# A one-core hybrid decoder layer: front order, scan pace and planner distances set anew

## The chip, the core and the metric

One core of a Trainium2 chip runs one layer. The time is that of the device in microseconds, from one launch; lower is better. PE is the matrix engine (TensorE), PEld its weight loads, DVE, ACT and POOL are the vector, scalar and general engines, and SP issues nearly all DMAs.

## The reference

The input is x with 1024 positions of 1024 values, float32. One projection by w_in feeds two mixers that run side by side; their outputs are gated, added and projected.

```python
h = rms_norm(x, norm_w)
q, k, v, z_a, xbc, z_s, dt_raw, gate_logits = split(h @ w_in)
y_a = diff_attention(q, k, v) * silu(z_a)      # 8 heads, two softmax maps of 64 dims each, causal
xs, B, C = split(silu(causal_conv4(xbc)))      # 2048 + 512 + 512 channels
y_s = ssd_chunked(xs, softplus(dt_raw), A, B, C, D)   # 32 heads, 4 groups, 8 chunks of 128
y_s = gated_group_rms_norm(y_s, z_s)
merged = sigmoid(g_a) * (y_a @ w_proj_attn) + sigmoid(g_s) * (y_s @ w_proj_ssd)
out = x + merged @ w_out
```

In the attention each map takes the row softmax of its scores, and the second, times a learned lambda, is taken from the first before the product with v. The scan carries a state of 128 x 512 per group from chunk to chunk.

## The kernel before

**Arithmetic.** Float32 accuracy comes from pairs: every operand is held as a rounded high part and a remainder, and a product is three matmuls (high x high, high x low, low x high; `steps3`, `mm3`). A weight therefore costs a load, a copy on ACT (high part) and a subtraction on DVE or POOL (low part). Large products are done by a scheme with seven block products instead of eight; it needs sums and differences of blocks of both operands.

**Stages.** The front makes what the scan needs: `FRONT_ORDER` is a string of blocks that PE works through. y is the first half of a z projection (`z_first`, tiles pmz), and "z16" one block product of the second kind of z projection (`z_part`: pair 1, product 6; tiles pz). c is a pair of 128-column blocks of the conv channels and g one of the gates (`front_pair`: PSUM banks fX, fY, fZ); e is the first part of a gate pair (`gate_first`), which makes the later g pair of the same number short (order `REST`, five products of 12 matmuls instead of seven). d is the dt projection. Then come eight heads (`att_proj`, tiles pma) with the attention blocks, then the remaining gates (pg), the output projections of both mixers (`products`: px, py, pz) and the last projection (`final`: poa to pod).

**The scan and the attention run between.** A group of the scan starts when its conv blocks (four of x, one of B, one of C) and its z rows lie in DRAM. Each chunk (`ssd_chunk`) is a chain through all engines; its PE work (px, pc, pb, pO, pS, pD, py) falls between the projection's matmuls. `qk_stack` transposes a half of a head's q and k, and `att_core` starts the blocks of 128 query rows one after another (`att_block`: scores sc, transposes pa, product av, transpose pya). The scores use 64 of the 128 rows of PE.

**What sets the order.** The program is written by a planner. `Plan` keeps a clock `pl.t` and a busy time for each engine; each piece of work is a generator that yields the time at which it wants to go on, and the projections (`bulk`) fill the rest. Every instruction is emitted when the planner's clock reaches it, so the planner's costs and distances set the order in which instructions stand on each engine, and buffers are handed out by its estimate of when they come free. On the chip each engine works through its own list in order and waits on semaphores.

**Names that the change touches.** `PACE` (line 35) is the distance between the starts of two chunks of the scan (line 1496); `ZSUMS` (line 40) gives the times at which the sums of weight blocks start (`weight_sums` on POOL: the first two for the z weights, absolute; the third for w_out, counted from the end of the heads' projections, line 2151). Line 831 starts `qk_stack` after a head's half is projected, line 900 parts two attention blocks, lines 205 and 221 to 226 hold costs of matmuls, line 235 the time until a result is out of PE, line 105 how far an engine's queue may run ahead.

**Weights of a front pair.** Four raw tiles (`rawf`, four buffers of the pool `raw`) are loaded by SP. POOL makes differences and sums of them (`s3`, `rawf`), and each of seven (five) pieces is split by ACT and DVE or POOL into a weight tile `wp`; there are nine of these. The next pair's loads can start only when the four raw buffers come free.

**Partial sums of z.** `z_part` gets `keep`: where the next block of the order is a product of the same pair, its partial sums (`zu`, `zv`, `zc`) stay in SBUF; otherwise they are stored to `zc_d` and loaded again.

Of the kernel before, what the change touches and what calls it, by code (L numbers as in the profile page):

```python
# [31 lines left out]
C_DT = 9216  # L32
C_GATE = 9248
NBIG, NW, NRAW, NMID, NSM = 17, 9, 4, 16, 8
PACE = 19.5
FRONT = 12
SLOW = 32.0
FRONT_ORDER = "y0 e6 y1 e0 e4 c6 e2 d0 c20 z06 c16 z07 z05 g0 c2 z04 c0 z16 z03 g2 z17 z15 z14 c4 z13 c8 g8 c14 g6 c22 g10 c12 g4 c10 c18"
REST = (("t2", 6), ("b22", 3), ("t3", 7), ("t1", 5), ("t4", 4))
ZSUMS = (75.0, 182.0, 11.0)  # L40
WPOOL = 3
NEARLY = 48
FINAL = (("b11", 1), ("t1", 5), ("t2", 6), ("t3", 7), ("b21", 2), ("b22", 3), ("t4", 4))
NFIN = 4 * len(FINAL)
HOP = 0.12
DBG = 0
INF = float("inf")

# [36 lines left out]
class Plan:  # L85
# [8 lines left out]
    def op(self, eng, cost, after, shared=False):  # L94
# [3 lines left out]
        if shared:  # L98
            self.e["L"] = s + cost
        return s + cost + HOP  # L100

    def spawn(self, gen, at=None):
        self.tasks.append([self.t if at is None else at, gen])

    def room(self, eng, ahead=0.2):
        while self.e[eng] > self.t + ahead:
            yield self.e[eng] - ahead

# [37 lines left out]
def tile_hybrid_layer(ctx: ExitStack, tc: tile.TileContext, x, norm_w, w_in, q_norm_w, k_norm_w,  # L146
# [29 lines left out]
    pl = Plan()  # L176
# [7 lines left out]
    def bigt(shape, dt=F32, name="b"):  # L184
        return big.tile(shape, dt, tag="b4", name=name)
# [16 lines left out]
        return hpool.tile([P, KB, S], F32R, tag="h", name=name)  # L202


    lag = [0.0135, 1.5]

    shape = [""]

    def mm(o, lhsT, rhs, start, stop, after=0.0, **kw):
        nc.tensor.matmul(o, lhsT=lhsT, rhs=rhs, start=start, stop=stop, **kw)  # L210
        n, m = rhs.free_size(), lhsT.free_size()
        now = "c" if rhs.dtype == F32 and m <= 64 else "r" if rhs.dtype != F32 and lhsT.shape[0] <= 64 else ""
        if rhs.dtype == F32:
            c = 0.058 if now else max(4 * n / 2400, 0.215)
        elif now:
            c = max(n / 4800 + lag[0] / 2, 0.0545)
        else:
            c = max(n / 2400 + lag[0], 0.057 if m <= 64 else 0.107)
        c += 0.089 * (now != shape[0])
        shape[0] = now  # L220
        pl.t = max(pl.t, after) + c

# [2 lines left out]
        pl.t = max(pl.t, after) + 0.108  # L225

    def pe_done():
        return pl.t + 0.2

    def mm3(o, ah, al, bh, bl, first, last):  # L230
        mm(o, ah, bh, first, False)
# [8 lines left out]
    def act(o, i, f, after, **kw):  # L240
        nc.scalar.activation(o, i, f, **kw)  # L241
        if f in (AF.Silu, AF.Exp) and f != table[0]:
            table[0] = f
            pl.op("A", 1.3, after)
        c = 0.83e-3 * i.free_size() + (0.052 if in_ps(i) else 0.093) + 0.093 * (("accum_out" in kw) + any(not isinstance(kw.get(i, 0.0), float) for i in ("scale", "bias")))
        return pl.op("A", c, after)

    def tt(o, a, b, op, after, eng="V"):
        (nc.vector if eng == "V" else nc.gpsimd).tensor_tensor(out=o, in0=a, in1=b, op=op)  # L249
        n = o.free_size()  # L250
        if eng == "G":
            return pl.op("G", 0.095 + (1.85e-3 if op == ALU.mult else 2.3e-3) * n, after, True)
        sb = not in_ps(a, b)
        return pl.op("V", 0.07 + 0.07 * sb + 1.042e-3 * n, after, sb)

    def stt(o, a, s, b, op0, op1, after):
        nc.vector.scalar_tensor_tensor(out=o, in0=a, scalar=s, in1=b, op0=op0, op1=op1)  # L257
        sb = not in_ps(a, b)
        return pl.op("V", 0.07 + 0.07 * sb + 1.042e-3 * o.free_size() + (0.0 if isinstance(s, float) else 0.06), after, sb)
# [105 lines left out]
    ORDER1 = []  # L365
    for e in FRONT_ORDER.split():
        ORDER1.append((e[0], int(e[1:])))
# [220 lines left out]
    def w_next(n):  # L588
        i = used[0]
        used[0] += n  # L590
        return list(range(i, i + n))
# [47 lines left out]
    def form_evac(t):  # L639
# [10 lines left out]
        def split(f, src, at):  # L650
# [6 lines left out]
            for kp in range(2):  # L657
                yield from pl.room("V")
                at = tt(forms_t[f, 1, kp][0][:, :, cs], src[:, 2 * kp:2 * kp + 2], forms_t[f, 0, kp][0][:, :, cs],
                        ALU.subtract, at - HOP if kp else at)  # L660
            ready["formed", f, t] = at
# [35 lines left out]
    def prep_h(t):  # L697
# [28 lines left out]
        for i in range(2):  # L726
            hs = slice(i * 512, i * 512 + 512)
            at = stt(xt[:, hs], xt[:, hs], rs, nwb[i], ALU.mult, ALU.mult, at - HOP if i else at)
            nt.append(at)
# [10 lines left out]
    def h_evac(t, half, pt, kt, at):  # L740
# [5 lines left out]
        if t >= 4:  # L746
# [5 lines left out]
            b = b2[t][0][:, half * 4:half * 4 + 4]  # L752
            t1 = act(b, src, AF.Copy, max(at - HOP, pl.t))
            sums12[t, half] = (b, t1)
# [39 lines left out]
    def att_proj(h):  # L794
        ids = w_next(KB)
        ks = []
        for _ in range(4):
            ks.append((yield from pl.get(heads)))
        v = bigt([P, NT, P], name=f"v{h}")
        zg = bigt([P, NT, P], name=f"zg{h}")  # L800
        kk = [bigt([P, S], F32R, name=f"kk{h}{i}") for i in range(2)]
        hd[h] = (v, zg, kk, ks)
        lefts[h] = [NT, {}]
        qk = []
        for ts in ((0, 1), (2,), (3,), (4,), (5,), (6,), (7,)):
            pms = []
            for t in ts:
                k = yield from pl.get(trs, first=True)
                pms.append((mmt(f"pma{h}{t}"), k))
                if t % 2 == 0:  # L810
                    km = yield from pl.get(qkm)
                    qk.append([midt([P, 2, 256], name=f"qk{h}{t}"), km, 0])
            if FRONT == 16 and h == HEADS - 1 and ts[0] == NT - 1:
                pl.spawn(h_done())
            for kb in range(KB):
                yield from w_need(ids[kb])
                for t, (pm, k) in zip(ts, pms):
                    yield from steps3(pm, hblk(kb, t), wide(ids[kb]), kb == 0, kb == KB - 1)
                    if kb == KB - 1:
                        pl.spawn(att_evac(h, t, pm, k, qk[-1][0][:, t % 2, :], qk[-1]), pe_done())  # L820
                if ts[0] == NT - 1:
                    w_done(ids[kb])
            if ts[-1] % 4 == 3:
                pl.spawn(qk_stack(h, ts[0] // 4, qk), pl.t + 3.0)
                qk = []

    def h_done():
# [27 lines left out]
    def qk_stack(h, half, qk):  # L855
        v, zg, kk, _ = hd[h]
        cs = slice(half * 512, half * 512 + 512)
        while len(qk[0]) < 5 or len(qk[1]) < 5 or "consts" not in ready:
            yield pl.t + 0.2
        yield max(qk[0][3:] + qk[1][3:] + [ready["consts"]])  # L860
        kq = yield from pl.get(bigs)
        q = bigt([P, 2, 512], F32R, name=f"q{h}{half}")
        done = []
        for isk in range(2):
            k = yield from pl.get(trs)
            pt = trt(f"pq{h}{half}{isk}")
            for i in range(4):
                tp(pt[:, i * P:(i + 1) * P], qk[i // 2][0][:, i % 2, isk * P:(isk + 1) * P])
            if isk:
                for c in qk:  # L870
                    qkm.give(c[1], pl.t + 0.1)
            at = pe_done()
            yield at
            if isk:
                t1 = act(kk[0][:, cs], pt, AF.Copy, at)
                yield t1
                t1 = tt(kk[1][:, cs], pt, kk[0][:, cs], ALU.subtract, t1)
            else:
                t1 = act(q[:, 0], pt, AF.Copy, at, scale=wqk_c)
                yield t1  # L880
                t1 = stt(q[:, 1], pt, wqk_c, q[:, 0], ALU.mult, ALU.subtract, t1)
            done.append(t1)
            trs.give(k, t1)
        pl.spawn(att_core(h, half, (q, kq)), max(done))

    def att_core(h, half, q):
        for qb in range(half * 4, half * 4 + 4):
            while bigs.avail(1 + half) > pl.t:
                a = bigs.avail(1 + half)
                yield a if a < INF else pl.t + 0.2  # L890
            pk = [bigs.take() for _ in range(1 + half)]
            pl.spawn(att_block(h, qb, pk, q))
            yield pl.t + 0.6

    def att_block(h, qb, pk, q):
        v, zg, kk, ks = hd[h]
# [7 lines left out]
        def soft(m):  # L904
            p = bigt([P, S], name=f"p{h}{qb}{m}") if qb >= 4 else pboth[:, m]
            nms, t1 = [], 0.0
            for i, (j, e) in enumerate(cols):
                while len(scs) <= i:
                    yield pl.t + 0.1
                sc, k, at = scs[i]  # L910
                at = max(at, t1 - HOP)
                yield at
# [40 lines left out]
        yield at  # L953
        at = stt(pr[0][:, 0:n], pr[1][:, 0:n], cc, pr[0][:, 0:n], ALU.mult, ALU.add, at - HOP)
        if qb >= 4:
# [513 lines left out]
    def ssd_core(g):  # L1469
# [20 lines left out]
        for c in range(NT):  # L1490
# [4 lines left out]
            pl.spawn(ssd_chunk(g, c, state, abs_))  # L1495
            yield pl.t + (PACE if bigs.avail(3) <= pl.t or 'setup' in ready else SLOW)

# [429 lines left out]
    def out_block(c, ob, r, h, ps, cell, at, free=None):  # L1927
# [15 lines left out]
        if c == 2 and ob >= 4:  # L1943
            mids.give(km[1], at)
            rows[ob + r - 4, h] = (gt, km[0], at)
            if DBG: print("  rows",ob+r,h,round(at,1),round(pl.t,1),"V",round(pl.e["V"],1),"G",round(pl.e["G"],1),"A",round(pl.e["A"],1))
            return
# [186 lines left out]
    def bulk():  # L2134
# [3 lines left out]
        for i in range(2):  # L2138
            pl.spawn(weight_sums(i, w_in, C_ZS + i * 1024, ZSUMS[i]))
        for n, (kind, i) in enumerate(ORDER1):  # L2140
# [9 lines left out]
        pl.spawn(fill())  # L2150
        pl.spawn(weight_sums(2, w_o, 0, pl.t + ZSUMS[2]))
        yield from gates()
# [74 lines left out]
```

## Time and profile before

| | |
|---|---|
| median of 3 runs | 1575.51 us (1575.27 to 1576.5) |
| the profiled execution | 1579.94 us |
| its span, first to last instruction | 1578.2 us |
| granted clock of PE, mean of the span | 0.995 |
| DMA | 287.46 MB, mean 182 GB/s |

The profile is one execution. Its page gives each engine's busy time, the span in 40 slices and the chain that ended last; further views group instructions, list who waited for whom, show a stretch in order of time, or sum busy times in chosen stretches. "[0.88 <-ACT wp L241]" behind an instruction says that its engine stood idle for 0.88 us before it and that ACT's write of wp ended the wait. PE's instructions overlap, so a block of equal matmuls is timed from the start of the first to the start of the next block. Nearly all matmuls are recorded under line 210, the helper `mm`.

### The profile page before, as it was taken

The numbers are of one execution on the slowest core, as the hardware profiler recorded it, in microseconds if no ns is written. First come the engines' busy times: TensorE is split into PE (matmuls) and PEld (weight loads), VectorE is DVE, ScalarE is ACT, GpSimd is POOL, SyncE is SP. The second block draws the span as 40 slices with busy tenths as digits, with TensorE's granted clock in tenths as the row PEclk, the third lists the DMA queues.
The fourth block names the chain that finished last, engine by engine and source line by source line (L and its number), as shares of the span: only waits on it lengthen the run. The fifth ranks groups of instructions, "written<-read, shape, count | busy, mean of one in ns | idle before, by whom it ended". The sixth has DMA issues, their size and how long they took to land.

```text
span 1578.2 us, 26112 instructions
## 1 busy us (share of the span) xinstructions
PE 1551.3 (98%) x8562; PEld 1256.0 (80%) x8562; DVE 1152.4 (73%) x2111; ACT 897.0 (57%) x2209; POOL 775.7 (49%) x902
## 2 busy tenths in 40 slices
PE   7989999999999999999999999999999999999999
PEld 5866888888888788778887877787878788888887
DVE  5767868577688778766778677876456687888985
ACT  7653434567555575676667666666546464443350
POOL 3264366344556553546684645464765744222005
PEclk9999999999999999999999999999999999999999
DMA  6475698753544453425473323343445797798846
GB/s 226 149 248 178 225 303 286 249 184 121 157 143 145 153 150 115 134 64 155 140 225 98 106 89 106 92 148 94 160 147 179 234 306 265 256 320 270 307 136 220
DMA packets 254825, 287.46 MB, mean 182 GB/s; under 512 B 18391, under 2 KB 162528, under 8 KB 254690
## 3 DMA queue, kind: packets, MB, share of 16 engines
q1 hardware_dynamic: 254686, 285.79, 56.3%
q8 instruction: 68, 1.11, 0.3%
q14 instruction: 67, 0.55, 0.1%
q10 hardware_dynamic: 4, 0.00, 0.0%
HBM read 196.47 MB, written 89.26 MB: 181 GB/s over the span
## 4 chain that ended last, share of the span: by engine, by line
PE 90%; ACT 3%; DMA 2%; DVE 2%; issue 1%; POOL 1%; SPq 0%; POOLq 0%; DVEq 0%; ACTq 0%
PE pma L210 22%; PE pz L210 10%; PE py L210 6%; PE fYc L210 6%; PE fXc L210 4%; PE sc L210 4%; PE av L210 4%; PE fZc L210 4%; PE px L210 4%; PE pO L210 3%; PE pg L210 3%; PE fYg L210 2%; PE pmz L210 2%; PE pa L224 2%; PE poz L210 1%; PE poy L210 1%
## 5 line engine op out<-in xcount | busy, mean ns | idle before, releaser
L210 PE MATMUL pma<-w,hH 128*128 128x512 f32 x1024 | 346.3, 407 | 0.3 <-DVE y L257 0.3
L210 PEld LDWEIGHTS pma<-w,hH 128*128 128x128 f32 x1024 | 187.0, 189 | 39.2 <-issue 4.5
L210 PE MATMUL pma<-w,hL 128*128 128x512 f32 x512 | 209.4, 409 | 0.0
L241 ACT ACTIVATE w<-raw 128x512 fp32r<-128x512 f32 (+1 forms) x166 | 101.1, 627 | 53.6 <-DMA raw<-wf_d 23.1
L249 DVE TENSOR_TENSOR w<-raw,w 128x512 fp32r<-128x512 f32 (+1 forms) x134 | 106.0, 808 | 27.6 <-ACT w L241 25.4
L210 PEld LDWEIGHTS pma<-w,hL 128*128 128x128 f32 x512 | 96.6, 189 | 21.7 <-issue 5.3
L241 ACT ACTIVATE p<-p,nm 128x256 f32<-128x256 f32 (+7 forms) x128 | 98.3, 773 | 25.8 <-DVE nm L914 24.9
L210 PE MATMUL fYc<-ft,wp 128*128 128x512 f32 x432 | 107.0, 395 | 3.5 <-DVE fu L249 1.8
L249 POOL TENSOR_TENSOR rawf<-rawf,rawf 128x512 f32<-128x512 f32 x54 | 70.7, 1310 | 79.4 <-DVE wp L249 36.2
L210 PEld LDWEIGHTS fYc<-ft,wp 128*128 128x128 f32 x432 | 81.8, 190 | 22.1 <-DVE fu L249 2.4
L210 PE MATMUL pz<-w,ft 128*128 128x512 f32 x384 | 90.3, 392 | 0.0
L241 ACT ACTIVATE wp<-rawp 128x512 fp32r<-128x512 f32 x72 | 44.3, 626 | 76.4 <-POOL rawp L249 18.8
L914 DVE CUSTOM_DVE_ANT_0 p<-sc,maskb 128x512 f32<-128x512 f32 (+3 forms) x128 | 69.8, 586 | 24.1 <-PE sc L210 24.0
L210 PEld LDWEIGHTS pz<-w,ft 128*128 128x128 f32 x384 | 71.6, 188 | 15.1 <-DVE w L249 0.4
L241 ACT ACTIVATE ab<-ab,nac 128x128 f32<-128x128 f32 x256 | 78.4, 391 | 5.0 <-POOL ab L1479 4.7
L249 POOL TENSOR_TENSOR rawp<-rawp,rawp 128x512 f32<-128x512 f32 x36 | 52.0, 1454 | 57.1 <-DVE wp L249 50.0
L249 POOL TENSOR_TENSOR os<-os,os 128x512 f32<-128x512 f32 x48 | 67.2, 1400 | 23.8 <-DMA os<-in_w_in_dram 19.6
L210 PEld LDWEIGHTS av<-v,at 128*128 128x128 f32 x576 | 72.1, 191 | 6.4 <-issue 1.5
L210 PE MATMUL av<-v,at 128*128 128x128 f32 x576 | 75.5, 276 | 0.3 <-ACT at L241 0.3
L281 POOL TENSOR_TENSOR rs<-rs,mhalf 128x4 f32<-128x4 f32 (+1 forms) x71 | 72.5, 1021 | 5.9
L945 POOL TENSOR_TENSOR rec<-s,mone 128x1 f32<-128x1 f32 x64 | 35.6, 557 | 76.9 <-ACT p L241 76.4
L210 PE MATMUL sc<-kk,q 64*128 64x512 f32 (+3 forms) x576 | 72.0, 367 | 0.0
(378 smaller groups left out, 4194.1 us busy)
## 6 DMA issues: line engine op xcount, KB each, us to landing
raw<-in_w_in_dram SPq DMA_DIRECT2D x104, 256.0 KB, 2.9
rawf<-in_w_in_dram SPq DMA_DIRECT2D x72, 256.0 KB, 3.9
ab<-act_d SPq DMA_DIRECT2D x32, 512.0 KB, 4.7
wf_d<-os SPq DMA_DIRECT2D x48, 256.0 KB, 5.1
cv_d<-cv SPq DMA_DIRECT2D x48, 256.0 KB, 3.5
raw<-wf_d SPq DMA_DIRECT2D x48, 256.0 KB, 3.6
t_d<-ts SPq DMA_DIRECT2D x24, 512.0 KB, 3.2
os<-in_w_in_dram SPq DMA_DIRECT2D x32, 256.0 KB, 4.5
```

Of the source, the lines that this page charges most:

```text
L210: nc.tensor.matmul(o, lhsT=lhsT, rhs=rhs, start=start, stop=stop, **kw)
L224: nc.tensor.transpose(out=o, in_=i, identity=ident if idn is None else idn)
L241: nc.scalar.activation(o, i, f, **kw)
L249: (nc.vector if eng == "V" else nc.gpsimd).tensor_tensor(out=o, in0=a, in1=b, op=op)
L281: nc.gpsimd.tensor_tensor(out=dst, in0=dst, in1=mhalf[:, 0:cols], op=ALU.pow)
L914: nc.vector.tensor_tensor_reduce(out=p[:, j:e], in0=sc[m][:, 0:e - j], in1=maskb[:, S - n + j:S - n + e], scale=-1.0, scalar=nms[i - 1] if ...
L945: nc.gpsimd.tensor_tensor(out=rec, in0=sums[1], in1=mone, op=ALU.pow)
```

## The change

Three tables of numbers and the front order change, and eight numbers that stood in the code get names. No matmul is added or removed.

```diff
-PACE = 19.5
+PACE = 18.0
-FRONT_ORDER = "y0 e6 y1 e0 e4 c6 e2 d0 c20 z06 c16 z07 z05 g0 c2 z04 c0 z16 z03 g2 z17 z15 z14 c4 z13 c8 g8 c14 g6 c22 g10 c12 g4 c10 c18"
+FRONT_ORDER = "y0 e6 y1 e0 e4 c6 e2 d0 c20 z06 c16 z07 z05 g0 c2 z04 c0 c10 z16 z03 g2 z17 z15 c4 z14 z13 c8 c14 g6 g8 c12 g4 g10 c22 c18"
-ZSUMS = (75.0, 182.0, 11.0)
+ZSUMS = (75.0, 182.0, 3.0)
+DONE = 0.2
+STACK = 2.0
+SPACE = 0.4
+AHEAD = 0.2
+DLAG = 1.5
+TURN = 0.089
+HALF = 0.05
-            c = 0.058 if now else max(4 * n / 2400, 0.215)
+            c = HALF if now else max(4 * n / 2400, 0.215)
-                pl.spawn(qk_stack(h, ts[0] // 4, qk), pl.t + 3.0)
+                pl.spawn(qk_stack(h, ts[0] // 4, qk), pl.t + STACK)
-            yield pl.t + 0.6
+            yield pl.t + SPACE
```

`DONE`, `AHEAD`, `DLAG` and `TURN` have the values of the numbers that they replace. `STACK` (3.0 before), `SPACE` (0.6) and `HALF` (0.058) have new ones. In the front, c10 moves from the last place but one to the place behind c0, c4 comes between z15 and z14, g8 goes behind g6, g10 behind g4, and c22 stands just ahead of c18. Each engine's list changes in order; SP's has 16 DMAs more, the partial sums of z15 that are stored and loaded again, and ACT's has two table loads less.

More of the change, by code (lines that the diff above doesn't have):

```diff
@@ L103, in spawn, with room @@
         self.tasks.append([self.t if at is None else at, gen])
-    def room(self, eng, ahead=0.2):
+    def room(self, eng, ahead=AHEAD):
         while self.e[eng] > self.t + ahead:
@@ L202, in hpt @@
         return hpool.tile([P, KB, S], F32R, tag="h", name=name)
-    lag = [0.0135, 1.5]
+    lag = [0.0135, DLAG]
     shape = [""]
@@ L218, in mm @@
             c = max(n / 2400 + lag[0], 0.057 if m <= 64 else 0.107)
-        c += 0.089 * (now != shape[0])
+        c += TURN * (now != shape[0])
         shape[0] = now
@@ L227, in pe_done @@
     def pe_done():
-        return pl.t + 0.2
+        return pl.t + DONE
     def mm3(o, ah, al, bh, bl, first, last):
```

## The prediction

> **What bounds the kernel now.** I read the page first: the busy shares, then the chain that ended last.
>
> ```profile
> span 1578.2 us, 26112 instructions
> PE 1551.3 (98%) x8562; PEld 1256.0 (80%) x8562; DVE 1152.4 (73%) x2111; ACT 897.0 (57%) x2209; POOL 775.7 (49%) x902
> PE 90%; ACT 3%; DMA 2%; DVE 2%; issue 1%; POOL 1%; SPq 0%; POOLq 0%; DVEq 0%; ACTq 0%
> ```
>
> TensorE is busy 98% of the span and nine tenths of the chain are its own instructions. The change adds and removes no matmul, so it can act in only two ways: through the time in which PE stands still, and through what a matmul loses because of the one ahead of it. The idle time is 1578.2 - 1551.3 = 26.9 us. Next I cut the span into stretches of 50 us, and then one longer stretch of the attention part.
>
> ```profile
> 0.00:50.00 50.00, 40.71 (x172) 30.64 (x173) 31.39 (x56) 38.62 (x71) 14.86 (x31) 0.93 0.62 205
> 50.00:100.00 50.00, 47.84 (x208) 38.37 (x207) 36.25 (x53) 28.73 (x66) 22.68 (x17) 1.00 0.55 181
> 100.00:150.00 50.00, 45.71 (x196) 34.20 (x195) 37.01 (x59) 16.96 (x31) 29.55 (x24) 0.97 0.72 227
> ...
> 200.00:250.00 50.00, 50.00 (x222) 41.30 (x221) 34.21 (x48) 20.35 (x37) 35.78 (x27) 1.00 0.95 313
> ...
> 500.00:550.00 50.00, 47.35 (x262) 38.40 (x261) 36.88 (x51) 26.74 (x53) 29.11 (x25) 0.97 0.47 144
> ```
> ```profile
> sum 500.00, PE 497.72 PEld 398.05 DVE 364.10 ACT 339.77 POOL 275.95; mean PE 99.54 PEld 79.61 DVE 72.82 ACT 67.95 POOL 55.19
> ```
>
> The columns are PE, PEld, DVE, ACT and POOL busy time, granted clock, DMA share and GB/s. At 200 to 250 us PE is full, 222 matmuls in 50 us. At 500 to 550 us, where the front ends, 2.65 us are missing and the clock is 0.97. The last row sums 600 to 1100 us, where attention and the scan run: 2.3 us idle in 500 us. Of the 26.9 us, 9.29 + 2.16 + 4.29 = 15.7 lie in the first 150 us, and there the PE order is unchanged: its first difference stands at the end of the block fZc0, where z16 (pz) starts at 265.78 us.
>
> ```profile
> 265.78 1.52 PE L210 MATMUL pz<-w,ft 128*128 128x512 f32 x6
> ```
>
> So what the change can win back sits around 540 us.
>
> **The stall near 540 us, the first term.** The waits of PE in 500 to 600 us, PE's timeline, and the engines that feed it:
>
> ```profile
> PE fXc L210 <- DVE wp L249: 1.8, 1, 1.8
> PE fXc L210 <- ACT wp L241: 0.9, 1, 0.9
> PE fXc L210 <- ACT fc L241: 0.5, 1, 0.5
> ```
> ```profile
> 535.16 1.15 PE L210 MATMUL pO<-xdt,ab 128*64 128x64 f32 x32
> 537.19 0.50 PE L210 MATMUL fXc<-hH,wp 128*128 128x512 f32 x1 [0.88 <-ACT wp L241]
> 537.53 0.40 PE L210 MATMUL fXc<-hL,wp 128*128 128x512 f32 x1
> 539.70 1.22 PE L210 MATMUL fXc<-hH,wp 128*128 128x512 f32 x2 [1.77 <-DVE wp L249]
> 540.72 0.63 PE L210 MATMUL fXc<-hL,wp 128*128 128x512 f32 x1
> ...
> 542.42 0.81 PE L210 MATMUL fXc<-hH,wp 128*128 128x512 f32 x2
> ...
> 549.46 2.88 PE L210 MATMUL fYc<-ft,wp 128*128 128x512 f32 x12
> 552.18 2.88 PE L210 MATMUL fZc<-ft,wp 128*128 128x512 f32 x12
> ```
> ```profile
> 530.83 2.10 SPq L270 DMA_DIRECT2D rawf<-in_w_in_dram  x4
> ```
> ```profile
> 529.75 1.29 POOL L249 TENSOR_TENSOR wp<-rawf,wp 128x512 fp32r<-128x512 f32 x1
> 535.31 1.28 POOL L249 TENSOR_TENSOR s<-rawf,rawf 128x512 f32<-128x512 f32 x1 [4.27 <-DMA rawf<-in_w_in_dram]
> ```
> ```profile
> 531.11 0.67 DVE L249 TENSOR_TENSOR fu<-fc,fYg 128x512 f32<-128x512 f32 x1
> 535.27 0.69 DVE L249 TENSOR_TENSOR fc<-fc,fYg 128x512 f32<-128x512 f32 x1 [0.41 <-PE fYg L210]
> 538.97 0.67 DVE L249 TENSOR_TENSOR wp<-rawf,wp 128x512 fp32r<-128x512 f32 x1
> ```
> ```profile
> 540.00:545.00 5.00, 5.00 (x19) 3.99 (x19) 1.43 (x3) 3.54 (x7) 3.69 (x5) 0.72 0.14 52
> ```
>
> This is the pair c10, behind the short gate pair g4. A short pair has five products of 12 matmuls instead of seven. The four raw buffers come free only when POOL has split g4's last piece (529.75); then the loads of c10 are issued (530.83 to 532.93) and land from 535.3. The lower half of c10's first weight is written at 538.97, behind four other DVE rows that follow g4's last sum (535.27), and PE starts in earnest at 539.70. A steady matmul takes (552.18 - 549.46)/12 = 0.227 us. The two gaps are 0.88 + 1.77 = 2.65 us. Behind them six matmuls take 542.42 - 539.70 = 2.72 us instead of 6 x 0.227 = 1.36: the clock row (0.72) shows why. The stall costs 2.65 + 1.36 = **4.0 us**.
>
> The Trainium skill, "TensorE: Matmul & The Clock Gate", section "What's actually happening", says the clock halves after about one idle window of 3.4 us, windows running freely. This trace shows the halving after two gaps of 0.88 and 1.77 us with two matmuls between. By the rule's letter the stall would cost 2.65 us alone.
>
> The new front order takes c10 out of this place and runs it right behind c0. PE, before and then now, at c0's end (fXc10 is c10's first bank, pz61 the products z16):
>
> ```order
> L210 MATMUL fZc0_2358<-hL_115,wp81_2367 128x512
> L210 MATMUL fZc0_2358<-hH_114,wp81_2367 128x512
> L210 MATMUL pz610_2532<-w48_2421,ft20_204 128x512 x2
> L210 MATMUL pz610_2532<-w48_2421,ft22_206 128x512
> L210 MATMUL pz610_2532<-w49_2430,ft20_204 128x512 x2
> L210 MATMUL pz610_2532<-w49_2430,ft22_206 128x512
> ```
> ```order
> L217 MATMUL fZc0_2358<-hL_115,wp81_2367 128x512
> L217 MATMUL fZc0_2358<-hH_114,wp81_2367 128x512
> L217 MATMUL fXc10_2519<-hH_114,wp82_2465 128x512
> L217 MATMUL fXc10_2519<-hL_115,wp82_2465 128x512
> L217 MATMUL fXc10_2519<-hH_114,wp82_2465 128x512 x2
> L217 MATMUL fXc10_2519<-hL_115,wp82_2465 128x512
> ```
>
> 84 matmuls of c10 move ahead of z16, about 19 us, so z16's summed weights have that much more time. What stands behind g4 now is g10. The question is whether g10 starves as c10 did. DVE shows it, before and then now: wp170 and wp163 are the first weights of the pair behind g4, and fc<-fc,fYg4 is g4's last sum.
>
> ```order
> L249 TENSOR_TENSOR fc_5031<-fc_5031,fYg4_5029 128x512
> L257 SCALAR_TENSOR_TENSOR cv1_5035<-tail_4915,cols1_109,cv1_5035 128x2
> L249 TENSOR_TENSOR pO07_5158<-pO07_5158,xn07_5042 128x512
> L257 SCALAR_TENSOR_TENSOR cv1_5035<-tail_4915,cols1_109,cv1_5035 128x3
> L249 TENSOR_TENSOR xn07_5042<-pO07_5158,zc07_5170 128x512
> L249 TENSOR_TENSOR wp170_5210<-rawf820_5147,wp170_5210 128x512
> ```
> ```order
> L256 TENSOR_TENSOR fu7_4914<-fc_4819,fYg4_4817 128x512
> L256 TENSOR_TENSOR wp163_4905<-rawf810_4832,wp163_4905 128x512
> L256 TENSOR_TENSOR fu7_4914<-fu7_4914,fZg4_4818 128x512
> L256 TENSOR_TENSOR fu6_4855<-fu6_4855,fZg4_4818 128x512
> L264 SCALAR_TENSOR_TENSOR cv1_4733<-tail_4809,cols1_109,cv1_4733 128x3
> L264 SCALAR_TENSOR_TENSOR cv1_4823<-fZc12_4610,cols1_109,cv1_4823 128x511
> L256 TENSOR_TENSOR fc_4819<-fc_4819,fYg4_4817 128x512
> ```
>
> The first weight moves from five rows behind g4's last sum to five rows ahead of it, right behind fu7<-fc. In the trace those two sums lie 535.27 - 531.11 = 4.2 us apart, so the weight should be there before g4's last product ends. c22 behind g10, the next close place, has its first weight two rows ahead of g10's last sum. I take the whole stall as gone: **-4.0 us**. The 0.5 us wait of fXc on fc I leave as it is:
>
> ```profile
> 563.11 2.45 ACT L241 ACTIVATE ab<-ab,nac 128x128 f32<-128x128 f32 x8
> ...
> 566.65 0.58 ACT L241 ACTIVATE fc<-fXc 128x512 f32<-128x512 f32 x1
> ```
>
> it comes when eight exponentials of the scan (2.45 us) stand ahead of the copy on ACT, which the new order does not exclude; bounds 0.5 either way.
>
> **Turns of the array, the second term.** The scores (sc) use 64 of the 128 rows; around each run of them PE loses time.
>
> ```profile
> 1012.27 0.39 PE L210 MATMUL pma<-w,hH 128*128 128x512 f32 x1
> 1012.59 0.97 PE L210 MATMUL sc<-kk,q 64*128 64x512 f32 x6
> 1013.48 0.50 PE L210 MATMUL pma<-w,hH 128*128 128x512 f32 x1
> ```
> ```profile
> 840.04 0.62 PE L210 MATMUL pma<-w,hH 128*128 128x512 f32 x2
> 840.59 1.67 PE L210 MATMUL sc<-kk,q 64*128 64x512 f32 x12
> 842.18 0.50 PE L210 MATMUL pma<-w,hL 128*128 128x512 f32 x1
> ```
>
> From start to start a run of 6 costs 1.21 - 0.227 = 0.98 us, a run of 12 costs 2.14 - 2 x 0.227 = 1.69. Joining two saves 2 x 0.98 - 1.69 = 0.28 us. The smaller distances of the attention blocks (0.6 to 0.4) join some runs and part others; PE's rows have 74 runs before and 69 now. One of them, head 0, before and now (sc0000 and sc0010 are the two maps of block 0, sc0100 and sc0110 those of block 1):
>
> ```order
> L210 MATMUL sc0000_6091<-kk00_5642,q00_5995 128x128
> L210 MATMUL sc0010_6092<-kk00_5642,q00_5995 128x128
> L210 MATMUL pma05_6018<-w91_5699,hH_114 128x512
> L210 MATMUL sc0100_6108<-kk00_5642,q00_5995 128x256
> L210 MATMUL sc0110_6109<-kk00_5642,q00_5995 128x256
> ```
> ```order
> L217 MATMUL sc0000_6018<-kk00_5588,q00_5922 128x128
> L217 MATMUL sc0010_6019<-kk00_5588,q00_5922 128x128
> L217 MATMUL sc0100_6027<-kk00_5588,q00_5922 128x256
> L217 MATMUL sc0110_6028<-kk00_5588,q00_5922 128x256
> L217 MATMUL sc0100_6027<-kk01_5589,q00_5922 128x256
> ```
>
> The pma row no longer parts the blocks 0 and 1. Five runs fewer at 0.28 are **-1.4 us**.
>
> **What is added, the third term.** "No instruction added" holds for PE, not for SP: c4 now stands between z15 and z14, so z15's partial sums go to DRAM and come back, 8 stores and 8 loads of 256 KB, 4.2 MB. At 313 GB/s (the row at 200 us) that is 13 us of the DMA engines, hidden beside PE's work on c4; if that cover failed, a PSUM bank would wait for its load, 3.9 us as for the weights:
>
> ```profile
> rawf<-in_w_in_dram SPq DMA_DIRECT2D x72, 256.0 KB, 3.9
> ```
>
> Partial sums already go out and come back around other z steps before, and no wait of PE names them, so I take nothing. HALF (0.058 to 0.05) is only the planner's own cost of a small matmul. The scan's pace (19.5 to 18.0), the earlier stacks (3.0 to 2.0) and the closer blocks put PE's rows nearer behind the DVE and ACT rows that they need. The trace cannot show that wait; the 2.3 us idle of 600 to 1100 us bound it: all of it may go, or it may double. I take **+1.0 us**, under half of it more, since two of the distances shrink by a third and DVE is 73% busy there. The earlier w_o sums (11.0 to 3.0 behind the last head) are read by the last stage alone: nothing.
>
> Sum: -4.0 - 1.4 + 1.0 = -4.4 us. The profiled execution took 1579.94 us (span 1578.2 and what lies around it), so 1575.5 of its kind; the median of the runs is 1575.51, 4.4 lower than the profiled one, and with the same difference it becomes **1571.1 us**. A measurement here tells about 0.2%, 3.2 us, from no change.
>
> **Rivals.** (a) The starvation moves instead of going: g8 behind g6 or g10 behind g4 waits. For it: both are still pairs behind a short pair, and a load that misses its time there stops PE at once. Against it: the DVE rows above. It gives back 2.65 to 4.0 us: 1573.8 to 1575.1. (b) The half clock is not paid in ordinary runs, or not in all: the slow stretch followed gaps of under 2 us in one execution, and the profiled one is 4.4 us above the median. Then only 2.65 is won there and the time is 1575.51 - 2.65 - 1.4 + 1.0 = 1572.5; this is also what the page's rule gives. (c) Slower: crowding of DVE in 600 to 1100 us. With the scan at 18.0 and blocks at 0.4, DVE's queue runs late by more than PE has other work for. Three gaps as long as the 1.77 us one, each with a slow stretch of 1.36, are 9.4 us and give 1575.51 - 5.4 + 9.4 = 1579.5. It decides from about 8.6 us of new loss on; DVE at 73% and 2.3 us idle now speak against it. (d) More is won: the 0.5 us of fc and the 2.3 us go too, and no wait comes: 1575.51 - 5.4 - 2.8 = 1567.3.
>
> **How the numbers follow.** Forecast 0.50, (a) 0.20, (b) 0.12, (c) 0.08, (d) 0.10. Faster by over 0.2% (below 1572.4) are the forecast and (d), 0.60; within it (a) and (b), 0.32; slower (c), 0.08. The range runs from 1566.8, just under (d), to 1576.0, above (a); (c) and the far ends are left out.
>
> **What would show it.** Right: no wait of fXc or fXg on wp of over 0.3 us between 500 and 580 us, and a granted clock of 1.00 there; PE idle in 600 to 1100 us of 2 to 5 us; shorter sums of PE idle by about 2.6 us in the front. Wrong: a new gap of over 1 us with a clock row below 0.9 anywhere behind 266 us, or a wait of PE on a bank that z14 or z13 holds while its partial sum is loaded.

## The result and the profile after

The changed kernel takes **1562.65 us** (median of 6 runs, 1562.19 to 1563.96), the kernel before 1575.24 us beside it (6 runs, 1572.81 to 1576.5). The ratio is 0.9924 (0.9912 to 0.9937): 12.6 us faster, 4.2 us beyond the fast end of the range. The profiled execution took 1562.57 us.

A word on line numbers: the changed kernel stands seven lines lower. Where the text ahead names lines 831, 900, 221 to 226 and 235, these are its lines; in the kernel before they are 824, 893, 214 to 219 and 228. In the rows below `mm` is L217, the transposes L231, ACT's copies L248, DVE's and POOL's sums L256.

The page of the changed kernel: its span, its busy times, and its chain by engine.

```profile
span 1560.8 us, 26193 instructions
PE 1540.5 (99%) x8562; PEld 1252.8 (80%) x8562; DVE 1146.5 (73%) x2113; ACT 894.3 (57%) x2207; POOL 774.9 (50%) x900
PE 95%; DMA 1%; ACT 1%; DVE 1%; issue 0%; POOL 0%; SPq 0%; DVEq 0%; ACTq 0%; POOLq 0%
```

PE's share of the chain rises from 90% to 95%; its idle time falls from 26.9 us to 1560.8 - 1540.5 = 20.3 us, and the same 8562 matmuls keep it busy for 10.8 us less. Both of these mix two things, since the first profile of the kernel before had a slow start: its clock was 0.93 in the first 50 us. A second profile of the same program (the first experiment below) starts like this, by the stretches of 50 us:

```profile
0.00:50.00 50.00, 40.06 (x181) 30.03 (x182) 34.50 (x60) 40.35 (x73) 14.92 (x31) 1.00 0.67 222
```

It did 181 matmuls there instead of 172, and its span is 1571.6 us: **6.6 us between two executions of one program**. I compare the changed kernel with this second one from here on. The busy times from 151 us to the end, of the kernel before in its second profile and then of the changed kernel:

```profile
151.00:1571.60 1420.60, 1410.67 (x7963) 1148.55 (x7961) 1043.08 (x1931) 808.81 (x2038) 709.21 (x831) 1.00 0.56 180
```
```profile
151.00:1560.80 1409.80, 1404.05 (x7961) 1147.94 (x7959) 1032.95 (x1932) 806.29 (x2035) 706.32 (x828) 1.00 0.57 185
```

The second number less the third is PE's idle time behind the start: 9.9 us before, 5.75 after. Some 3.3 us of either lie behind the last matmul, so of 6.6 us that can be won 4.2 are gone. The views of PE's waits in the same stretches say which, of the kernel before (second profile) and of the changed kernel; the columns are us in total, times, longest:

```profile
PE fXc L217 <- DVE wp L256: 1.4, 1, 1.4
PE fXc L217 <- ACT wp L248: 0.9, 1, 0.9
PE pya L231 <- DVE y L264: 0.8, 2, 0.5
PE pa L231 <- DVE p L264: 0.6, 1, 0.6
PE pod L217 <- DVE xr L264: 0.6, 1, 0.6
PE pb L231 <- ACT at L248: 0.5, 1, 0.5
PE fXc L217 <- ACT fc L248: 0.5, 1, 0.5
PE py L217 <- DVE u L256: 0.5, 1, 0.5
PE pq L231 <- DVE qk L256: 0.4, 1, 0.4
PE av L217 <- ACT at L248: 0.3, 1, 0.3
PE pma L217 <- DVE y L264: 0.3, 1, 0.3
```
```profile
PE py L231 <- ACT xn L248: 0.9, 1, 0.9
PE pod L217 <- DVE xr L264: 0.6, 1, 0.6
PE fYg L217 <- DVE fu L256: 0.5, 1, 0.5
PE pO L217 <- DVE ab L256: 0.5, 1, 0.5
```

The list shrinks from eleven rows to four. The stall of c10 (the two rows of fXc on wp) is gone and so are all waits of the attention part. The sums over 600 to 1300 us, before (second profile) and after, show the latter best:

```profile
sum 700.00, PE 697.17 PEld 561.27 DVE 488.05 ACT 451.57 POOL 406.93; mean PE 99.60 PEld 80.18 DVE 69.72 ACT 64.51 POOL 58.13
```
```profile
sum 700.00, PE 699.98 PEld 567.12 DVE 492.11 ACT 454.99 POOL 408.62; mean PE 100.00 PEld 81.02 DVE 70.30 ACT 65.00 POOL 58.37
```

Idle there: 2.83 us before, **0.02 us after**, although DVE, ACT and POOL are each a little busier. In the front, the row of the changed kernel for the place where the stall stood, and its three small new waits in PE's timeline:

```profile
500.00:550.00 50.00, 50.00 (x256) 41.26 (x256) 31.27 (x48) 28.89 (x56) 27.65 (x23) 1.00 0.47 144
```
```profile
429.06 1.15 PE L217 MATMUL pO<-xdt,ab 128*64 128x64 f32 x32 [0.48 <-DVE ab L256]
434.27 0.66 PE L231 MATMUL py<-ident,xn 128*128 128x128 f32 x4 [0.89 <-ACT xn L248]
497.65 2.56 PE L217 MATMUL fYg<-ft,wp 128*128 128x512 f32 x10 [0.49 <-DVE fu L256]
```

### The profile page after: what moved, and what is told of

Read it like the earlier page. It is cut to its first block, busy times and chain, and to the rows that moved or that the text cites. A ratio compares the mean times of both kernels' runs of the same rounds, so it can differ in the third digit from the quotient of the medians.

```text
span 1560.8 us, 26193 instructions
## 1 busy us (share of the span) xinstructions
PE 1540.5 (99%) x8562; PEld 1252.8 (80%) x8562; DVE 1146.5 (73%) x2113; ACT 894.3 (57%) x2207; POOL 774.9 (50%) x900
## 4 chain that ended last, share of the span: by engine, by line
PE 95%; DMA 1%; ACT 1%; DVE 1%; issue 0%; POOL 0%; SPq 0%; DVEq 0%; ACTq 0%; POOLq 0%
PE pma L217 23%; PE pz L217 11%; PE py L217 6%; PE fYc L217 6%; PE sc L217 4%; PE av L217 4%; PE fXc L217 4%; PE px L217 4%; PE fZc L217 4%; PE pO L217 3%; PE pg L217 3%; PE fYg L217 3%; PE pmz L217 2%; PE pa L231 2%; PE poz L217 1%; PE fZg L217 1%
## 5 line engine op out<-in xcount | busy, mean ns | idle before, releaser
L217 PE MATMUL pma<-w,hH 128*128 128x512 f32 x1024 | 344.9, 407 | 0.0
L217 PEld LDWEIGHTS pma<-w,hH 128*128 128x128 f32 x1024 | 186.2, 189 | 40.8 <-issue 6.6
L217 PE MATMUL pma<-w,hL 128*128 128x512 f32 x512 | 207.9, 406 | 0.0
L248 ACT ACTIVATE w<-raw 128x512 fp32r<-128x512 f32 (+1 forms) x166 | 100.9, 631 | 57.2 <-DMA raw<-wf_d 21.1
L256 DVE TENSOR_TENSOR w<-raw,w 128x512 fp32r<-128x512 f32 (+1 forms) x136 | 107.3, 808 | 29.0 <-ACT w L248 28.2
L217 PEld LDWEIGHTS pma<-w,hL 128*128 128x128 f32 x512 | 96.7, 189 | 20.3 <-issue 2.9
L217 PE MATMUL fYc<-ft,wp 128*128 128x512 f32 x432 | 106.1, 392 | 2.4 <-DVE ft L256 1.8
L248 ACT ACTIVATE p<-p,nm 128x256 f32<-128x256 f32 (+7 forms) x128 | 98.1, 770 | 17.8 <-DVE nm L921 15.9
L256 POOL TENSOR_TENSOR rawf<-rawf,rawf 128x512 f32<-128x512 f32 x54 | 71.8, 1329 | 64.2 <-issue 20.6
L217 PEld LDWEIGHTS fYc<-ft,wp 128*128 128x128 f32 x432 | 80.4, 188 | 20.4 <-DVE ft L256 2.2
L248 ACT ACTIVATE wp<-rawp 128x512 fp32r<-128x512 f32 x72 | 44.2, 627 | 81.7 <-PE py L217 23.5
L217 PE MATMUL pz<-w,ft 128*128 128x512 f32 x384 | 90.5, 392 | 0.3 <-DVE w L256 0.3
L256 POOL TENSOR_TENSOR os<-os,os 128x512 f32<-128x512 f32 x48 | 65.1, 1357 | 43.0 <-DMA os<-in_w_out_dram 19.5
L217 PEld LDWEIGHTS pz<-w,ft 128*128 128x128 f32 x384 | 71.6, 188 | 15.4 <-DVE w L256 0.7
L256 POOL TENSOR_TENSOR rawp<-rawp,rawp 128x512 f32<-128x512 f32 x36 | 53.2, 1491 | 53.8 <-DVE wp L256 40.1
L248 ACT ACTIVATE ab<-ab,nac 128x128 f32<-128x128 f32 x256 | 78.4, 397 | 2.2 <-POOL ab L1486 2.1
L217 PEld LDWEIGHTS av<-v,at 128*128 128x128 f32 x576 | 72.5, 191 | 5.1 <-issue 1.1
L248 ACT ACTIVATE wp<-rawf 128x512 fp32r<-128x512 f32 x100 | 60.3, 623 | 27.6 <-POOL rawf L256 24.1
L217 PE MATMUL av<-v,at 128*128 128x128 f32 x576 | 75.4, 276 | 0.0
L217 PE MATMUL sc<-kk,q 64*128 64x512 f32 (+3 forms) x576 | 70.8, 366 | 0.0
```

## The experiments

The question was where 12.6 us come from when the prediction found 4.4. The theories: the gain is the sum of its parts (front, pace, distances, sums), each worth something alone; or one part brings it; or it belongs to the order that all the numbers make together, and to no number. Each kernel computes everything. All are in the table; the idle time is PE's behind 151 us, from the same row as above (the expectations count it without the 3.3 us behind the last matmul).

| kernel | median, us | ratio to before | idle, us |
|---|---|---|---|
| before, profiled again | 1573.35, one run | | 9.9 |
| changed | 1562.65 | 0.9924 (0.9912 to 0.9937) | 5.75 |
| before + front order | 1573.89 | 1.0001 (0.999 to 1.0012) | 12.8 |
| before + pace | 1588.11 | 1.0089 (1.0073 to 1.0105) | 18.7 |
| before + distances | 1589.74 | 1.0101 (1.0085 to 1.0118) | 23.7 |
| changed, old front order | 1585.25 | 1.0071 (1.0054 to 1.0087) | 18.5 |
| changed, old pace | 1569.67 | 0.9968 (0.9955 to 0.9981) | 10.5 |
| changed, old distances | 1570.82 | 0.9975 (0.9964 to 0.9986) | 10.4 |
| changed, old sums | 1563.11 | 0.993 (0.9915 to 0.9945) | 6.0 |
| changed, pace 18.2 | 1572.86 | 0.9987 (0.9975 to 0.9999) | 12.05 |
| changed, blocks at 0.45 | 1584.61 | 1.0053 (1.0035 to 1.0072) | 17.8 |
| before, pace 19.3 | 1573.36 | 1.0002 (0.9987 to 1.0017) | 11.7 |
| before, blocks at 0.55 | 1573.13 | 0.999 (0.9979 to 1.0002) | 10.3 |
| before, c10 moved alone | 1574.53 | 1.0006 (0.9996 to 1.0015) | 11.2 |
| before + pace, weights on DVE | 1585.5 | 1.0081 (1.0066 to 1.0096) | 19.7 |
| changed, weights on DVE | 1581.16 | 1.005 (1.0034 to 1.0067) | 14.35 |

### The kernel before, profiled again

No edit of its numbers.

> All numbers are those of the kernel before; the instructions stand as they did. The two profiles differ by 17.4 us of span, the medians by 12.6, and 6.0 us of PE's loss lie in the first 150 us, where both kernels have the same PE order. Theory A (the start is chance: its waits meet the clock's window sooner or later): this second profile of the same program gives another loss there, 3 us or more away from the first one's 24 us, and the stall near 540 us is there again with a gap of over 1 us. Rival B (the start became shorter through the change): the first 150 us repeat within 1 us.

Its time was 1573.35 us. The stall of c10 came again, with nearly the same numbers (PE's timeline, and the busy times of two stretches of 5 us):

```profile
531.11 0.50 PE L217 MATMUL fXc<-hH,wp 128*128 128x512 f32 x1 [0.88 <-ACT wp L248]
...
533.21 1.22 PE L217 MATMUL fXc<-hH,wp 128*128 128x512 f32 x2 [1.36 <-DVE wp L256]
```
```profile
530.00:535.00 5.00, 2.76 (x14) 1.88 (x11) 2.44 (x5) 2.81 (x6) 3.22 (x5) 0.80 0.70 258
535.00:540.00 5.00, 5.00 (x22) 4.01 (x21) 2.63 (x4) 4.04 (x8) 3.77 (x4) 0.86 0.00 0
```

The clock goes below 1 here as in the first profile, so the slow stretch behind the stall is no accident of one execution. Most of what differs between the two executions lies in the first 151 us: the second did 24 matmuls more there (7963 behind them against 7987), some 5.4 of the 6.6 us at 0.227 us each.

### Each part alone

The kernel before with the new front order:

```diff
-FRONT_ORDER = "... z04 c0 z16 z03 g2 z17 z15 z14 c4 z13 c8 g8 c14 g6 c22 g10 c12 g4 c10 c18"
+FRONT_ORDER = "... z04 c0 c10 z16 z03 g2 z17 z15 c4 z14 z13 c8 c14 g6 g8 c12 g4 g10 c22 c18"
```

With the new pace:

```diff
-PACE = 19.5
+PACE = 18.0
```

With the new distances:

```diff
-STACK = 3.0
-SPACE = 0.6
-HALF = 0.058
+STACK = 2.0
+SPACE = 0.4
+HALF = 0.05
```

> Only the new front order; pace, distances and sums as before. Theory A: the stall near 540 us goes (2.65 us of gaps and 1.36 us of slow clock), 70 runs of scores instead of 74 save 1.1 us, small waits of 600 to 1300 us stay: 5 us less, ratio 0.9968. Rival C (the front order carries the whole gain): ratio 0.992, 12 us less. Rival D (the front order only moves the stall): ratio 0.9985 to 1.000.

> Only the scan's pace, 18.0 for 19.5. Theory A: the stall near 540 us stays, 75 runs of scores instead of 74, some of the small waits behind 600 us go or come: ratio 0.999 to 1.001. Rival E (a faster pace is what emptied the waits between 600 and 1300 us, about 5 us of PE's loss): ratio 0.997.

> Only the planner's distances: stacks 2.0 for 3.0, attention blocks 0.4 for 0.6, cost of a small matmul 0.05 for 0.058. Theory A: 72 runs of scores for 74, 0.6 us less; the prediction held that nearer rows bring new waits of 1 us, so ratio 1.000 to 1.001. Rival F (nearer rows take away the waits between 600 and 1300 us, 5 us): ratio 0.997.

**No part alone brings anything.** The front order alone is worth nothing: c10's stall is gone, but other waits stand in its place, as PE's waits from 151 to 600 us show:

```profile
PE fYg L217 <- DVE fu L256: 1.9, 1, 1.9
PE py L231 <- ACT xn L248: 1.4, 1, 1.4
PE fXc L217 <- ACT fc L248: 0.8, 1, 0.8
```

The pace and the distances alone cost 14 and 15.5 us. With the distances alone, one wait shows the way in which it happens: PE's row, POOL's timeline ahead of it, and the stretch's busy times.

```profile
828.44 0.80 PE L217 MATMUL pma<-w,hH 128*128 128x512 f32 x1 [5.11 <-POOL w L256]
```
```profile
820.62 1.29 POOL L256 TENSOR_TENSOR ts<-ts,ts 128x512 f32<-128x512 f32 x1
821.99 1.61 POOL L256 TENSOR_TENSOR ts<-ts 128x512 f32<-128x512 f32 x1
...
823.70 1.09 POOL L1486 TENSOR_SCALAR_AFFINE_SELECT ab<-ab 128x1024 f32<-128x1024 f32 x1
...
827.11 1.27 POOL L256 TENSOR_TENSOR w<-raw,w 128x512 fp32r<-128x512 f32 x1
```
```profile
825.00:830.00 5.00, 1.56 (x4) 1.17 (x5) 1.73 (x5) 3.75 (x13) 4.50 (x7) 0.57 0.46 127
```

The remainder of a head's weight (`w<-raw,w`) stands on POOL behind work of the scan (`ab`) and sums of the scan's outputs (`ts`), which the output projection needs later; PE's list has the matmul that needs it next, and nothing behind that matmul may pass it. 5.1 us are lost, and a clock of 0.57 comes on top. Over the whole of 600 to 1300 us PE is idle for 700 - 685.79 = 14.21 us in this kernel:

```profile
600.00:1300.00 700.00, 685.79 (x4470) 551.01 (x4469) 478.96 (x1064) 445.32 (x1354) 396.54 (x581) 0.99 0.43 138
```

### Each part undone

Each is the changed kernel with the old number or numbers of one part put back.

The last of them, the sums:

```diff
-ZSUMS = (75.0, 182.0, 3.0)
+ZSUMS = (75.0, 182.0, 11.0)
```

> The changed kernel with the old front order; pace, distances and sums new. The parts alone gave 1.0001 (front), 1.0089 (pace) and 1.0101 (distances), the whole 0.9924. Theory G (the parts only fit together; each set of numbers makes another order, and the whole is one that has no long gap): the stall of c10 near 540 us is back, 3 to 4 us, and at least one gap of over 1 us stands between 600 and 1200 us: ratio 0.998 to 1.010. Theory H (pace and distances together make the gain behind 600 us, whatever the front): ratio 0.995.

> The changed kernel with the scan's pace of 19.5. Its order has 70 runs of scores (69 in the changed one). Theory G: at least one new gap of over 1 us behind 400 us, ratio 0.996 to 1.010. Theory I (front order and distances carry it, the pace is not needed): ratio 0.992 to 0.994.

> The changed kernel with stacks 3.0, blocks 0.6 and the cost of a small matmul 0.058 as before; front, pace and sums new; 75 runs of scores. Theory G: at least one new gap of over 1 us, ratio 0.996 to 1.010. Theory J (front order and pace carry it): ratio 0.993 to 0.995, the 6 runs of scores more cost 1.7 us.

> The changed kernel with the sums of the w_out blocks at 11.0 behind the last head instead of 3.0. The sums come last, so the order ahead of about 1190 us should stand as in the changed kernel, unless it differs in between. My step gave this part nothing: ratio 0.992 to 0.993, and the 366.6 us from the last matmul of the heads to the end within 0.5 us. Theory G would allow up to 2 us more in that stretch.

The sums are worth nothing, as predicted. Without the new front the kernel is 22.6 us slower, without the new pace 7.0, without the new distances 8.2 (differences of the medians). These are no shares: they sum to 38 us where there are 12.6, and alone the same three cost 0, 14 and 15.5 us. The parts do not add.

One thing came otherwise than expected. With the old front order put back, c10 stands behind g4 again, yet its stall does not return: this kernel's list of waits has no fXc on wp, and the row of the place is full. PE waits at an earlier place instead, for DVE's `ab`:

```profile
500.00:550.00 50.00, 50.00 (x281) 41.09 (x280) 35.78 (x55) 25.70 (x50) 25.96 (x23) 1.00 0.51 152
```
```profile
475.48 1.15 PE L217 MATMUL pO<-xdt,ab 128*64 128x64 f32 x32 [3.06 <-DVE ab L256]
```

The distances alone do the same to the old front order: no wait of fXc on wp, and 3.05 us on `ab` at 477.83 us. So c10's place alone does not make its stall; the planner's distances make or unmake it as well.

### Small steps from the changed kernel and from the one before

Two from the changed kernel, then two from the one before:

```diff
-PACE = 18.0
+PACE = 18.2
```
```diff
-SPACE = 0.4
+SPACE = 0.45
```
```diff
-PACE = 19.5
+PACE = 19.3
```
```diff
-SPACE = 0.6
+SPACE = 0.55
```

> The changed kernel with the pace 18.2 instead of 18.0, 69 runs of scores as before. Theory K (the numbers pick one order among many, and the changed kernel's has hardly a gap; any small step picks another): PE idle behind 151 us grows from 2.4 us to 5 or more, ratio to the kernel before 0.995 to 1.005. Theory L (the numbers act by their direction: a faster pace is better): ratio 0.992 to 0.9935.

> The changed kernel with the attention blocks 0.45 apart instead of 0.4; 74 runs of scores for 69. Theory K: new gaps, PE idle behind 151 us of 5 us or more, ratio 0.995 to 1.005. Theory L: ratio 0.993 to 0.994, the 5 runs of scores more cost 1.4 to 2.0 us.

> The kernel before with the pace 19.3 instead of 19.5. Theory K: other gaps than before, idle behind 151 us anywhere from 4 to 16 us, ratio 0.997 to 1.009. Theory L: within 0.15% of the kernel before, a little faster if faster paces help.

> The kernel before with the attention blocks 0.55 apart instead of 0.6; 74 runs of scores as before. Theory K: ratio anywhere from 0.997 to 1.009, with other gaps. Theory L: within 0.15% of the kernel before.

From the changed kernel a step of 0.2 us in the pace costs 10 us, and 0.05 us between attention blocks costs 22 us. From the kernel before, steps of the same size cost nothing that can be measured. Both theories of the expectations (K and L) had allowed that, so only the two steps from the changed kernel tell them apart, and they speak for K. A distance of 0.05 us is far shorter than any instruction in these rows; what it changes is the order of the lists. In the kernel with blocks at 0.45 one gap near the end holds a good part of the loss (PE, then ACT, then DVE, then the busy times):

```profile
1502.26 1.22 PE L217 MATMUL poa<-w,mb 128*128 128x512 f32 x2 [8.20 <-DVE w L256]
```
```profile
1498.56 0.63 ACT L248 ACTIVATE hH<-mm 128x512 fp32r<-128x512 f32 x1 [9.66 <-DVE mm L256]
...
1500.65 0.61 ACT L248 ACTIVATE w<-raw 128x512 fp32r<-128x512 f32 x1
```
```profile
1501.52 0.68 DVE L256 TENSOR_TENSOR w<-raw,w 128x512 fp32r<-128x512 f32 x1
```
```profile
1500.00:1505.00 5.00, 2.75 (x7) 2.17 (x8) 4.93 (x9) 4.47 (x10) 0.00 (x0) 0.50 0.16 52
```

Here it is ACT, behind a DVE that is busy for 4.93 of 5 us: ACT's copy `hH<-mm` waits 9.66 us for DVE, the copy of the next weight stands behind it in ACT's list, DVE's half of that weight follows, and PE gets it 8.2 us late. Again the weight was not slow in itself; it stood behind something.

### One block moved, and the weights taken off POOL

After "each part alone" two narrower theories were left: that c10's place is all that the front needs, and that POOL, which makes every third remainder of the heads' weights, is the engine that spoils the other orders.

The kernel before with c10 moved:

```diff
-FRONT_ORDER = "... z04 c0 z16 z03 g2 z17 z15 z14 c4 z13 c8 g8 c14 g6 c22 g10 c12 g4 c10 c18"
+FRONT_ORDER = "... z04 c0 c10 z16 z03 g2 z17 z15 z14 c4 z13 c8 g8 c14 g6 c22 g10 c12 g4 c18"
```

The remainders of the heads' weights on DVE, once in the kernel before with pace 18.0, once in the changed kernel:

```diff
-WPOOL = 3
+WPOOL = 1000
```

> The kernel before with one edit in the front order: c10 stands behind c0 instead of behind g4; all else as before, 77 runs of scores for 74. The prediction's first step: the stall of c10 (2.3 to 2.65 us of gaps and 1.36 us of slow clock) goes, and c18 behind g4 has its weights in time; the runs cost 0.8 us: ratio 0.997 to 0.998. Theory K: c18 or another block starves in c10's place, or gaps in the heads take the gain back: ratio 0.9985 to 1.005.

> The slower version with the pace 18.0 alone (ratio 1.0089), with no low part of a head's weight on POOL: the number 3 that sends every third of them there is 1000, they all go to DVE. In its profile PE waited 3.8 us for POOL's w, which stood in POOL's list behind the sums ts. Theory M (POOL's list makes the long gap): the gap of pma on POOL's w is gone and no gap of over 2 us takes its place in the heads, ratio 0.998 to 1.003. Theory K without M: gaps as long stand elsewhere, ratio 1.005 to 1.012.

> The changed kernel with every low part of the heads' weights on DVE, 74 runs of scores for 69. Theory M: the changed kernel has no wait for POOL's w to lose, DVE gets about 20 splits of 0.7 us more, ratio 0.992 to 0.995. Theory K: a new order, new gaps, ratio 0.996 to 1.005.

c10's place alone is worth nothing either (1.0006). Its stall is gone, and a new gap comes earlier (PE's timeline):

```profile
493.86 1.98 PE L217 MATMUL pO<-xdt,ab 128*64 128x64 f32 x32 [4.32 <-POOL wp L256]
```

The row names POOL, whose last `wp` ends at 493.74 us. But these matmuls read `ab`, not `wp`, and DVE's row for `ab` ends at 493.71 us, 0.15 us ahead of PE's start. In the kernels with the distances alone and with the old front order back, PE's start at the same place lies 0.15 us behind `ab` too, while POOL's `wp` had ended 0.7 us ahead of it. So I take it as a wait for `ab`:

```profile
492.50 1.21 DVE L256 TENSOR_TENSOR ab<-ab,pc 128x1024 f32<-128x1024 f32 x1
```

With the pace alone, PE's largest waits from 600 to 850 us were these:

```profile
PE pma L217 <- POOL w L256: 3.8, 1, 3.8
PE sc L217 <- ACT at L248: 2.9, 1, 2.9
```

With the weights on DVE the first of them goes, but the time hardly moves (1.0089 to 1.0081): a wait of 4.1 us for `ab` (its row, too, names POOL's wp, but `ab` ends 0.15 us ahead of PE's start), 3.5 us on DVE (y) and 2.7 us on DVE (f0b) stand elsewhere. The changed kernel loses 18.5 us by the same edit, with 4.6 us of py on ACT and 2.7 us of px on DVE. So taking this work off POOL does not help: the late engine is POOL, ACT or DVE as the order has it. The edit is no clean test of POOL, though, since it also gives DVE 32 rows more (30 in the changed kernel) and so makes another order once again.

### What follows from all of them

The time follows PE's gaps. The changed kernel has the fewest (5.75 us) and is the fastest, the distances alone have the most (23.7 us) and are the slowest; in between the order of the table's two columns agrees but for kernels whose idle times, each of one execution, lie within 2.2 us of each other. Between those two ends the spans differ by 1590.7 - 1560.8 = 29.9 us, of which PE's idle time is 38.7 - 20.3 = 18.4 and its busy time 1552.0 - 1540.5 = 11.5 (both from the pages). The slower work is the clock: the mean granted clock is 0.992 in the one profile and 1.000 in the other, and 0.008 of 1590.7 us are some 12.7 us, about as much. But 3.5 us of it lie in the first 50 us (clock 0.93 there against 1.00), where the order of PE is the same. The other 8 us come with the 18 us of gaps, so a microsecond of gap cost 0.4 to 0.5 us of slower work here, as an average over long gaps.

What the change does is choose, out of many orders of the five in-order lists, one in which the lists hold back least of what PE needs next. That all neighbouring orders tried, but for the old sums, lack this is shown; why this combination has it, beyond the waits named above, is not, and I have no rule that would have found it without running it. No version beat the changed kernel; the old sums equal it.

## Why the prediction was wrong

- **The stall of c10 (-4.0 us): right about what happens there, not as a term of its own.** With all numbers changed it goes, and the row from 500 to 550 us is full at clock 1.00, as the prediction said would show it. The slow clock behind it came in the second profile too; by its two rows it cost (0.20 + 0.14) x 5 = 1.7 us there, for 1.36 in the prediction. Yet not every run pays it, so the rival "or not in all" holds in part: with this one slow stretch the second profile has a mean granted clock of 0.999, and 8 of the 65 runs of the kernel before that were timed beside the experiments have 1.000. With the front order alone, and with c10 moved alone, the gain was zero: the stall went and others came. That is the rival "the starvation moves", in places that it did not name (fYg on fu, py on xn, pO on ab instead of g8 or g10 on wp). And with the old front order the new distances took the stall away as well. Even in the changed kernel 0.89 + 0.49 + 0.48 = 1.9 us of new front waits stand against it; the idle time of 400 to 600 us falls by 0.97 us only, from 2.82 to 1.85. With the slow clock the front gave about 2.7 us between these two profiles.
- **The turns (-1.4 us): right in the count, open in size.** There are 69 runs of scores instead of 74. The rows of PEld that wait ahead of sc, before (second profile) and after, sum to 15.8 us in 51 and 15.3 us in 48, too small a difference to test 0.28 us a run:

```profile
PEld sc L217 <- issue: 13.6, 44, 0.4
...
PEld sc L217 <- DVE nm L921: 2.2, 7, 0.4
```
```profile
PEld sc L217 <- issue: 10.8, 35, 0.4
...
PEld sc L217 <- DVE nm L921: 4.5, 13, 0.4
```

- **The closer spacing (+1.0 us): this is the step that failed, in sign and in kind.** The prediction said: the numbers "put PE's rows nearer behind the DVE and ACT rows that they need", so small waits come, between 2.3 us won and 2.3 lost. In the changed kernel the waits of 600 to 1300 us went altogether, 2.81 us of idle time. With the distances alone the idle time there rose from 2.83 to 14.21 us instead, far past the upper bound. So the bound was no bound. Between the term of +1.0 and the 2.81 us that were won lie 3.8 us, the largest single part of the miss that the traces place. The prediction took the waits of the old order and asked how much longer they would grow; but the numbers do not stretch an order, they make another one, with other waits.
- **What was taken as nothing.** z15's partial sums that go out and come back, and the earlier sums for w_out, cost nothing: no wait of PE names the one, and 1563.11 us with the old sums answers for the other. The 0.5 us of fXc on fc went.
- **The sum.** Between the second profile of before and that of the changed kernel lie 10.8 us: 5.1 of idle time (25.4 to 20.3 by the pages) and 5.7 of busy time (1546.2 to 1540.5). Of the idle time 2.81 are the attention part, 0.97 the stretch from 400 to 600 us and 0.9 the first 151 us, where the order of PE is the same. Of the busy time 1.7 are the slow clock at c10, and 1.4 would be the turns at the predicted price; some 2.6 us I could not put to places. The medians differ by more, 12.6 us, and the granted clock has a part in that, since the kernel before has slow stretches more often (some of them in the first 150 us, as in its first profile, where the change does nothing): its 8 runs at a mean clock of 1.000 have a median of 1571.05 us, and the four of the changed kernel's six runs at 1.000 one of 1562.4. By this estimate from few runs, on several chips, 8.7 of the 12.6 us remain without slow stretches, where the prediction's terms without the slow clock add up to -2.65 - 1.4 + 1.0 = -3.05. The rival "more is won" was the right direction, at 1567.3 us still 4.7 us short.
- **The range.** Its fast end was that of the rival "more is won": the waits that the old trace showed from 500 to 1100 us gone, and nothing else. The price that a wait has beside its gap was counted for the one stall and left out for the rest; that this is where the 2.6 us without a place lie is not shown. The slower rival, at 1579.5 us, is what the pace or the distances do alone, at 1588 and 1590 us, and by way of POOL and ACT as well as DVE.

## What to carry to other kernels

Where a planner's numbers set the order of in-order lists, do not price such a number by the waits that it lengthens or shortens: compare the new order's list of waits, or run it, and try the numbers together, since parts that cost 0, 14 and 15.5 us alone here win 12.6 together. A kernel in that state is a point and no slope: after any other edit its numbers have to be searched again, and an edit's own worth cannot be read from the time of one such kernel. Two profiles of the program before, rather than one, tell what its start gives and takes by itself (6.6 us here).

## What the runs showed of the hardware

The length of the last gap alone does not tell whether the clock of PE falls. It fell after two gaps of 0.88 and 1.36 us close together (0.80, above), after one of 2.85 us with the pace alone (0.69), and after one of 1.80 us in the kernel before with pace 19.3:

```profile
1444.73 0.98 PE L217 MATMUL py<-hH,wp 128*128 128x512 f32 x3 [1.80 <-DVE u L256]
```
```profile
1445.00:1450.00 5.00, 5.00 (x16) 3.93 (x16) 2.76 (x5) 2.11 (x4) 1.71 (x2) 0.66 0.54 169
```

It did not fall after one of 2.13 us in the changed kernel with the old pace, nor after the 3.06 us with the old front order (the row of 475.48 us above); the 5 us around that gap:

```profile
475.00:480.00 5.00, 4.52 (x47) 3.90 (x48) 4.96 (x11) 1.73 (x4) 0.36 (x2) 1.00 0.64 204
```

The Trainium skill, "TensorE: Matmul & The Clock Gate", section "What's actually happening", puts the fall after an idle window of about 3.4 us. The gaps of 5.1 and 8.2 us here agree; those of 2.85, of 1.80 and of 0.88 + 1.36 us do not by the letter. Whether it is the share of idle time in a window that counts, or where the gap lies, was not tried.
